# A four-stage decoder trunk on one core: the mixer's work written out as one fixed order on all engines, a narrower overlap, and six more weights split ahead of time

## The chip, the cores and the metric

The kernel runs on one core of a Trainium2 chip. The metric is the device time of one execution in microseconds, the median of several runs; lower is better. The engines are PE (matrix products; PEld is its weight load, which overlaps), DVE (vector), ACT (scalar, with activation functions and running sums), POOL (a second vector engine) and SP, which here only issues DMAs. Each engine runs its own instructions in order, and a DMA that waits on SP holds up those behind it.

## The reference

512 tokens of 1024 channels go through two layers. Every sublayer has a norm in front and behind: x += norm(f(norm(x))), with norm the root-mean-square norm with a gain.

```python
for layer in range(2):
    h = rms_norm(x, mix_pre_g[layer])
    if layer == 0:
        m = pool_mixer(h, pool_w[0], pool_scale[0])      # causal averages over 2, 4, 8, 16 tokens, minus h;
    else:                                                 # then a 256x256 map for each of 4 channel groups
        q = h @ w_q[0]
        o = stick_breaking_attention(q, k, v)             # 16 heads of 64, cumulative products over keys
        m = o @ w_o[0]
    x = x + rms_norm(m, mix_post_g[layer])
    h = rms_norm(x, mlp_pre_g[layer])
    x = x + rms_norm(square(relu(h @ w_up[layer])) @ w_down[layer], mlp_post_g[layer])   # 4096 wide
    if layer == 0:
        k, v = split(rms_norm(x, kv_norm_g) @ w_kv)
```

All is float32, within a tolerance.

## The kernel before, in words

The tokens are four tiles of 128 (t = 0 to 3), the channels eight blocks of 128 (KC), a bank of PSUM holds 128 x 512 numbers and there are eight.

**Products of split operands.** To reach float32 accuracy, a large product takes three passes: each operand is a high part (`hi`, a copy rounded to the fast format, on ACT) and a low part (`lo`, the rest, a subtraction on DVE), and high·high, high·low and low·high are added (`mm3`, lines 255 to 257, and `up_block`, lines 609 to 611). A weight of 128 x 1024 is loaded by `weight` (line 114), copied on ACT (124) and subtracted on DVE (126). An activation tile is transposed on PE (326) and split into `xnh` and `xnl` (`split`, lines 234 and 235).

**Weights ahead of need.** `queue` holds the weights in the order of use; `fill` makes the next one when fewer than `ahead` = 4 wait. In the first MLP, `split_apart` (lines 163 to 186) does the split of 24 weights of the attention stage early: a raw load (176), a gain (135), a cast and a subtraction (184, 185), and one step later two stores into a DRAM tile `kept` (168). Each step advances every weight under way. `steps` (line 518) says after which of the 35 products of the first MLP a step runs. When such a weight is needed, `make` loads its two parts (195) and no split is needed. The raw copies take turns in a tile of three (`apart`), `spare` and `grow`.

**The mixer (lines 614 to 718).** Per tile t: `scaled` squares x on ACT with a running sum (238), takes the reciprocal root with DVE and POOL (`rstd`, lines 244 and 251), and scales x into `xs` (670). `pooled` multiplies by band matrices: eight blocks of 128 x 128 on the tile itself (679) and, for t > 0, eight on the tile before it (684), which bring in the up to 15 tokens that reach over the border; then `y` is copied out (687). `mixed` does the group maps (699), squares the result on ACT (238), multiplies it by the gain on DVE (280), and `add` takes the root and adds to x (286), squaring the new x on ACT. `normed` takes that root and makes `xn` (317). `need` transposes `xn`.

`MIX_ORDER` is the order in which the program text emits these steps; the scheduler then places the instructions of each engine by its own estimate of times, so that only dependencies, and the `issue_after` marks around the steps s, r and w, are given. PE starts with eleven products on zeros (620).

**The first MLP.** `mlp` takes the up products of the first four weights in halves: tokens 0 to 255 as soon as tiles 0 and 1 are transposed, tokens 256 to 511 behind tiles 2 and 3 (lines 551 to 559). The down product of 28 of the 32 blocks goes in five groups (2, 3, 3, 3, 3 pairs), each as seven products of combined operands (`Seven`, line 499): `left` combines activations on POOL (454), `right` combines weights on DVE (473), both are split, and `make(i + 2)` makes the operands two products ahead. The down weights of a group come in two loads, `load(0)` to `w1` and `load(1)` to `xn3` (438). The last four blocks go through `contract`.

**Attention, then the second MLP.** An order written out by hand (`ATT_ORDER`) interleaves projections, heads and the output product; the weights of the output, `o0` to `o7`, are split when they come. The second MLP is built as the first, without `split_apart`.

## Time and profile before

| | us |
|---|---|
| median of three runs | 977.46 (975.99 to 978.87) |
| the profiled execution | 977.16 |
| its span | 975.0 |
| PE busy | 950.8 |
| DVE busy | 709.3 |
| ACT busy | 567.8 |
| POOL busy | 142.3 |

The span runs from the first instruction to the last; 2.2 us lie around it. In rows of the timeline the columns are the start, the time of the row, engine, line, operation, output and inputs, and the number of instructions; in brackets stands the idle time just before and what ended it. Matrix products are pipelined, so the pitch of two rows, not the length of one, is what a product costs. In lists of waits the numbers are the sum, the count and the longest. The granted clock is 1 where PE runs at full speed.

Stages by their marks: the mixer and the first up products from 0 to 77 us, the first MLP to 380, attention to about 604, the output product's end and the second MLP behind it.

### The profile page before, as it was taken

What the parts mean: (1) busy time and instruction counts of PE and PEld (TensorE: products, weight loads), DVE (VectorE), ACT (ScalarE), POOL (GpSimd) and SP (SyncE); (2) the same over time, 40 slices, a digit from 0 to 9 for tenths busy, and PEclk for the clock granted to TensorE, in tenths of its full rate; (3) what the DMA queues carried; (4) which work ended last, traced back from release to release, by engine and by line L of the source; (5) the groups of instructions that cost most, each with busy time, mean ns of one, the idle gap of its engine ahead of it and who ended that gap; (6) DMA issues with size and microseconds to landing.
All of it is one profiled execution on the core that took longest, in us unless ns stands there. A gap on an engine that the chain in (4) does not pass through costs nothing.

```text
span 975.0 us, 12433 instructions
## 1 busy us (share of the span) xinstructions
PE 950.8 (98%) x4795; PEld 807.9 (83%) x4795; DVE 709.3 (73%) x769; ACT 567.8 (58%) x985; POOL 142.3 (15%) x107
## 2 busy tenths in 40 slices
PE   9899999999999999999999998999999999999997
PEld 7798878878888888989799987798888888888886
DVE  3764689796978967376567789875497785957856
ACT  4656788777777546555556574555455454444532
POOL 1102030320403105000000000312040310303003
PEclk8999999999999999999999999999999999999999
DMA  6262767968676540332353312143423324133012
GB/s 251 70 255 72 256 232 275 356 229 303 217 280 227 198 161 1 129 131 87 135 210 118 141 45 87 42 154 109 145 93 128 110 76 163 37 128 115 22 44 87
DMA packets 40092, 144.28 MB, mean 148 GB/s; under 512 B 4065, under 2 KB 4449, under 8 KB 40034
## 3 DMA queue, kind: packets, MB, share of 16 engines
q1 hardware_dynamic: 40034, 143.49, 41.6%
q8 instruction: 38, 0.62, 0.3%
q14 instruction: 20, 0.16, 0.0%
HBM read 116.21 MB, written 27.26 MB: 147 GB/s over the span
## 4 chain that ended last, share of the span: by engine, by line
PE 80%; DVE 8%; ACT 5%; DMA 3%; issue 3%; POOL 1%; DVEq 0%; POOLq 0%; SPq 0%; ACTq 0%
PE ps L499 23%; PE ps L610 12%; PE ps L611 12%; PE ps L609 12%; PE ps L255 4%; PE ps L256 4%; PE ps L257 4%; PE ps L869 2%; PE ps L859 1%; PE ps L699 1%; DMA xn<-in_wdn 1%; DVE w L126 1%; DMA kept<-apart 1%; ACT w L234 1%; PE ps L827 1%
## 5 line engine op out<-in xcount | busy, mean ns | idle before, releaser
L499 PE MATMUL ps<-w,a 128*128 128x512 f32 x1176 | 278.3, 389 | 2.8 <-DVE w L235 1.6
L610 PE MATMUL ps<-xnl,w 128*128 128x512 f32 (+1 forms) x712 | 261.5, 368 | 3.1 <-DVE xnl L235 3.1
L499 PEld LDWEIGHTS ps<-w,a 128*128 128x128 f32 x1176 | 220.5, 188 | 49.8 <-DVE w L235 2.5
L609 PE MATMUL ps<-xnh,w 128*128 128x512 f32 (+1 forms) x712 | 261.1, 368 | 0.4 <-ACT xnh L234 0.3
L611 PE MATMUL ps<-xnh,w 128*128 128x512 f32 (+1 forms) x712 | 261.3, 368 | 0.0
L610 PEld LDWEIGHTS ps<-xnl,w 128*128 128x128 f32 x712 | 134.1, 189 | 25.4 <-DVE xnl L235 3.7
L611 PEld LDWEIGHTS ps<-xnh,w 128*128 128x128 f32 x712 | 134.1, 188 | 22.3
L609 PEld LDWEIGHTS ps<-xnh,w 128*128 128x128 f32 x712 | 133.7, 188 | 22.7 <-ACT xnh L234 0.8
L126 DVE TENSOR_TENSOR w<-raw,w 128x1024 fp32r<-128x1024 f32 x71 | 91.8, 1293 | 66.7 <-ACT w L124 66.6
L124 ACT CAST w<-raw 128x1024 fp32r<-128x1024 f32 x71 | 74.5, 1050 | 107.1 <-PE ps L611 97.4
L508 DVE TENSOR_TENSOR y<-ps,y 128x512 f32<-128x512 f32 x124 | 83.4, 684 | 41.0 <-PE ps L499 41.0
L234 ACT CAST a<-r 128x768 fp32r<-128x768 f32 (+1 forms) x60 | 47.5, 793 | 63.2 <-PE ps L499 46.7
L454 POOL TENSOR_TENSOR s<-r 128x768 f32<-128x768 f32 (+1 forms) x10 | 20.6, 2057 | 371.2 <-ACT r L532 371.2
L234 ACT CAST w<-e 128x1536 fp32r<-128x1536 f32 (+1 forms) x30 | 42.0, 1398 | 46.9 <-DVE e L473 37.5
L235 DVE TENSOR_TENSOR a<-r,a 128x768 fp32r<-128x768 f32 (+1 forms) x60 | 59.9, 1003 | 12.3 <-ACT a L234 12.2
L280 POOL TENSOR_TENSOR y<-y,grow 128x512 f32<-128x512 f32 x12 | 18.8, 1563 | 317.4 <-ACT xn L238 317.4
L454 POOL TENSOR_TENSOR r<-r 128x768 f32<-128x768 f32 (+1 forms) x20 | 52.7, 2635 | 67.2 <-DVE a L235 66.4
L235 DVE TENSOR_TENSOR w<-e,w 128x1536 fp32r<-128x1536 f32 (+1 forms) x30 | 57.5, 1917 | 4.4 <-ACT w L234 4.2
L841 DVE TENSOR_TENSOR_SCAN e<-u,begin 128x1280 f32<-128x1280 f32 x16 | 45.1, 2822 | 12.6 <-ACT u L835 12.3
L135 ACT ACTIVATE apart<-apart,gc 128x128 f32<-128x128 f32 (+1 forms) x132 | 42.8, 405 | 0.0
L238 ACT ACTIVATE xn<-y 128x512 f32<-128x512 f32 (+1 forms) x25 | 15.4, 615 | 39.3 <-DVE y L361 39.2
L235 DVE TENSOR_TENSOR w<-xn,w 128x1536 fp32r<-128x1536 f32 (+1 forms) x20 | 33.0, 1650 | 6.1 <-ACT w L234 6.0
(128 smaller groups left out, 1490.7 us busy)
## 6 DMA issues: line engine op xcount, KB each, us to landing
raw<-in_wup SPq DMA_DIRECT2D x64, 512.0 KB, 3.8
w<-kept SPq DMA_DIRECT2D x48, 512.0 KB, 4.2
w<-in_wdn SPq DMA_DIRECT2D x8, 1536.0 KB, 6.7
kept<-wx SPq DMA_DIRECT2D x24, 512.0 KB, 5.2
xn<-in_wdn SPq DMA_DIRECT2D x8, 1536.0 KB, 7.3
kept<-apart SPq DMA_DIRECT2D x19, 512.0 KB, 3.2
raw<-in_wdn SPq DMA_DIRECT2D x8, 512.0 KB, 4.6
raw<-in_wo SPq DMA_DIRECT2D x8, 512.0 KB, 3.5
```

Of the source, the lines that this page charges most:

```text
L124: nc.scalar.copy(hi, raw)
L126: nc.vector.tensor_tensor(out=lo, in0=raw, in1=hi.bitcast(F32), op=ALU.subtract)
L135: nc.scalar.mul(c, c, gc[:, lo + k : lo + k + 1])
L234: latest["act"] = nc.scalar.copy(hi, src)
L235: latest["dve"] = nc.vector.tensor_tensor(out=lo, in0=src, in1=hi.bitcast(F32), op=ALU.subtract)
L454: sub = lambda out, x, y, op=ALU.subtract: nc.gpsimd.tensor_tensor(out=out, in0=x, in1=y, op=op)
L499: nc.tensor.matmul(bank, a[:, x, q, TS[t]], w[:, z, q], start=start and q == 0 and k == 0, stop=q == self.n - 1 and k == 2, skip_group_che ...
L508: nc.vector.tensor_tensor(out=part, in0=bank, in1=part, op=ALU.add)
L609: nc.tensor.matmul(pu[:, cols], wh[:, k, :], xnh[:, k, cols], start=k == 0, stop=False)
L610: nc.tensor.matmul(pu[:, cols], wh[:, k, :], xnl[:, k, cols], start=False, stop=False)
L611: nc.tensor.matmul(pu[:, cols], wl[:, k, :], xnh[:, k, cols], start=False, stop=k == KC - 1)
L841: nc.vector.tensor_tensor_scan(out=e[:, ::-1], data0=u[:, 1:][:, ::-1], data1=begin[:, ::-1], initial=0.0, op0=ALU.mult, op1=ALU.max,)
```

## The change

- `MIX_ORDER` is a new order, in halves of tiles, and it binds PE, ACT, DVE and POOL (`manual_schedule`). Its letters: q squares, x root and scaling, p pooling (tile, half), m maps, a sum, n norm, t transposes, r and w the gains on the maps, z products on zeros, F the next weight, u the first half of an up product. The first halves of the first four up products move into it (`early`), and `mlp` only does the rest of them. The products on zeros are 8, 6 and 6 instead of 11.
- The squares of x for tiles 1 to 3 are one instruction of 1024 instead of two of 512, with a memset of the second sum.
- The overlap with the tile before takes 16 columns instead of 128.
- `steps` is 1 to 33 without gaps instead of 2 to 30 without 17 and 24; o4 to o7 and the first two up weights of the second MLP are split apart too, without a gain, so 30 instead of 24.
- The raw load of a step is issued behind the latest of `latest["sp"]`, which is now also the store.
- The operands of the first group's first two products are issued behind the latest ACT and DVE work.
- A split up weight may use the fourth slot (`place`).

```diff
 MIX_ORDER = [
-    (w[0], int(w[1])) for w in "s0 r0 s1 w0 p0 p1 w1 s2 m0 s3 m1 p2 F3 n0 p3 t0 n1 t1 m2 F1 m3 n2 n3".split()
+    (w[0], [int(c) for c in w[1:]])
+    for w in """q0 z8 r z6 q1 x0 p00 p01 z6 x1 w0 p10 p11 w1 q2 m00 x2 q3 m01 a0 m10 m11 x3 p20 p21 n0
+    p30 a1 t00 t01 p31 F n1 m20 m21 F t10 t11 u0 a2 m30 F m31 u1 n2 a3 F t20 t21 u2 n3 F u3""".split()
 ]
...
-            fourth = count[0] % 4 == 0 and k[0] in "vkqo"
+            fourth = k[0] in "vkqo" and count[0] % 4 == 0 or k[0] == "up" and k[2] == GRP - 1
...
             for n, t in enumerate((hi.bitcast(F32), raw)):
-                nc.sync.dma_start(kept[k][n], t)
+                latest["sp"] = nc.sync.dma_start(kept[k][n], t)
...
-            nc.sync.dma_start(raw, src)
+
+            with tc.issue_after(latest["sp"].ins) if "sp" in latest else nullcontext():
+                nc.sync.dma_start(raw, src)
             going.append([k, 0, raw, None, scaled])
...
             if n == 1:
-                scaled(raw)
+                if scaled is not None:
+                    scaled(raw)
...
-            apart.extend(x for x in queue[n:] if x[0][0] != "o")
+            apart.extend(x for x in queue[n:] if x[0] not in [("o", c) for c in range(4)])
+            apart.extend((("up", 1, j), wup[1, j], None) for j in range(2))
...
-        def transpose(self):
-            for h in range(2):
+        def transpose(self, halves=range(2)):
+            for h in halves:
...
-        steps = [n for n in range(2, 31) if n not in (17, 24)] if l == 0 else []
+        steps = [n for n in range(1, 34)] if l == 0 else []
...
-        first = [(ps(), get(("up", l, j))) for j in range(n0)]
+        first = early[:]
+        while len(first) < n0:
+            first.append((ps(), get(("up", l, len(first)))))
         for j, (pu, w) in enumerate(first):
             if j == n0 - 1:
                 need(2, 3)
                 groups[0].load(1)
-            up_block(pu, w, slice(0, S // 2))
+            if j >= len(early):
+                up_block(pu, w, slice(0, S // 2))
+        early.clear()
...
-        for i in range(2):
-            groups[0].make(i)
+        with tc.issue_after(latest["act"].ins), tc.issue_after(latest["dve"].ins):
+            for i in range(2):
+                groups[0].make(i)
...
+        def busy(n):
+            for _ in range(n):
+                nc.tensor.matmul(pwarm, warm[:, :P], warm, start=True, stop=True)
...
+        def squares(t):
+            xs[t] = mp.tile([P, D], F32, tag=f"xs{t}", name=f"xs{t}")
+            sts[t] = keep.tile([P, 8], F32, tag=f"stat{t}", bufs=4, name=name("stat"))
+            if t == 0:
+                for n in range(2):
+                    square_sum(xt[t][:, NS[n]], xs[t][:, NS[n]], sts[t], n)
+            else:
+                nc.vector.memset(sts[t][:, 1:2], 0.0)
+                square_sum(xt[t], xs[t], sts[t], 0)
...
+        def pooled(t, h):
...
+                if t:
+
+                    n = max(WINDOWS)
                     nc.tensor.matmul(
-                            py[:, TS[c]], xs[t - 1][:, cs], band(2, cb // 2), start=False, stop=True
+                        py[:, c * P : c * P + n], xs[t - 1][:, cs], band(2, cb // 2)[:, :n], start=False,
+                        stop=True, skip_group_check=True,
                     )
...
+        def half_up(j):
+            early.append((ps(), get(("up", 0, j))))
+            up_block(*early[j], slice(0, S // 2))
+
+        steps = {
+            "q": squares, "x": scaled, "p": pooled, "m": mixed, "a": lambda t: ups[t].add(), "n": normed,
+            "t": transposed, "r": spread, "w": linear, "F": fill, "z": busy, "u": half_up,
+        }
+        on = mybir.EngineType
+        with tc.manual_schedule(engines={on.PE, on.Activation, on.DVE, on.Pool}):
+            for step, which in MIX_ORDER:
+                steps[step](*which)
```

More of the change, by code (lines that the diff above doesn't have):

```diff
@@ L617, in trunk @@
         nc.gpsimd.memset(warm, 0.0)
-        pwarm = ps()
-        for _ in range(11):
-            nc.tensor.matmul(pwarm, warm[:, :P], warm, start=True, stop=True)
         cst = mp.tile([P, 12 * P], F32, tag="cst", name="cst")
@@ new lines, in scaled @@
+        def scaled(t):
+            r = rstd(sts[t], 0)
+            for n in NS:
+                nc.vector.tensor_scalar(out=xs[t][:, n], in0=xt[t][:, n], scalar1=r, scalar2=None, op0=ALU.mult)
+        def pooled(t, h):
+            if not h:
+                ys[t] = mp.tile([P, D], F32, tag="y", bufs=2, name=f"y{t}")
+            py = ps()
+            for c in range(4):
+                cb = 4 * h + c
+                cs = slice(cb * P, (cb + 1) * P)
+                nc.tensor.matmul(
+                    py[:, TS[c]], xs[t][:, cs], band(0 if t == 0 else 1, cb // 2), start=True, stop=True,
+                    skip_group_check=True,
+                )
+                if t:
+                    n = max(WINDOWS)
@@ L706, in normed, with transposed @@
             pending[t] = ups[t]
[L708 to L718 removed]
+        def transposed(t, h):
+            ups[t].transpose((h,))
+            if h:
+                pending.pop(t)
+        def half_up(j):
[9 more added lines that the diff above has]
+                steps[step](*which)
     with tc.tile_pool(name="mlp0", bufs=1, reuse_waits="tile") as mp:
```

67 lines of the change are left out of this document (19 added, 48 removed).

## The prediction

> **What bounds the kernel now.** I read the page's busy shares first, then the waits of PE, then the timeline around each wait.
>
> ```profile
> PE 950.8 (98%) x4795; PEld 807.9 (83%) x4795; DVE 709.3 (73%) x769; ACT 567.8 (58%) x985; POOL 142.3 (15%) x107
> ```
>
> PE is idle for 975.0 − 950.8 = 24.2 us in all, so whatever removes no PE work can save at most this. The waits of PE, longest first, say who ends that idle time:
>
> ```profile
> PE ps L679 <- DVE xs L670: 4.5, 2, 3.9
> PE ps L610 <- DVE xnl L235: 3.1, 3, 2.1
> PE ps L256 <- DVE w L126: 2.1, 2, 1.9
> PE ps L499 <- DVE w L235: 1.6, 2, 1.0
> ```
>
> All four name DVE. Their places are the mixer (L679), the borders into the second MLP and of the last heads (L610, L256), and the first MLP (L499). The second thing that costs is the clock. In the windows the columns are length, busy time of PE, PEld, DVE, ACT and POOL, granted clock, DMA share and GB/s:
>
> ```profile
> 0.00:75.00 75.00, 68.36 (x431) 60.91 (x432) 44.63 (x74) 40.04 (x85) 7.92 (x19) 0.93 0.52 187
> 10.00:15.00 5.00, 4.41 (x21) 4.12 (x20) 4.05 (x10) 0.79 (x3) 0.51 (x1) 0.50 0.99 388
> 30.00:35.00 5.00, 3.52 (x22) 3.56 (x23) 4.34 (x7) 1.72 (x4) 0.55 (x1) 0.77 0.48 145
> 250.00:275.00 25.00, 25.00 (x112) 20.68 (x112) 25.00 (x21) 20.62 (x40) 9.77 (x4) 1.00 0.63 214
> ```
>
> So the mixer has 75 − 68.36 = 6.6 us of idle PE and two stretches at half clock, and in 250 to 275 us DVE is busy all the time.
>
> **Part 1: the mixer in a fixed order.** These PE rows give its pitches:
>
> ```profile
> 1.31 4.56 PE L620 MATMUL ps<-warm 128*128 128x512 bf16 x11 [1.31 <-POOL warm L617]
> 16.92 7.07 PE L699 MATMUL ps<-pw,y 128*128 128x256 f32 x32
> 23.83 0.39 PE L679 MATMUL ps<-cst,xs 128*128 128x128 f32 x2
> 24.05 0.39 PE L684 MATMUL ps<-cst,xs 128*128 128x128 f32 x2
> 31.48 0.46 PE L679 MATMUL ps<-cst,xs 128*128 128x128 f32 x2 [3.91 <-DVE xs L670]
> 36.75 1.91 PE L326 MATMUL ps<-ident,xn 128*128 128x128 f32 x16
> 57.62 0.28 PE L611 MATMUL ps<-xnh,w 128*128 128x256 f32 x1
> 57.74 0.28 PE L609 MATMUL ps<-xnh,w 128*128 128x256 f32 x1
> ```
>
> A 128-column pooling product takes 24.05 − 23.83 = 0.22 us, half a tile of the group maps 7.07/4 = 1.77, half a tile of transposes 4 × 0.11 = 0.44 (sixteen in 1.91, the last with its tail), a warm-up product 4.56/11 = 0.41. Half an up product is 24 × (57.74 − 57.62) = 2.88, and five of them from 57.40 on end the mixer's share at about 72. The other engines, in the same stage:
>
> ```profile
> 18.85 0.60 ACT L238 ACTIVATE xn<-ps 128x512 f32<-128x512 f32 x1
> 37.43 2.06 ACT L234 CAST xnh<-ps 128x512 fp32r<-128x512 f32 x4
> ```
>
> ```profile
> 19.57 0.69 DVE L280 TENSOR_TENSOR m<-ps,grow 128x512 f32<-128x512 f32 x1 [0.39 <-ACT xn L238]
> 35.60 1.23 DVE L126 TENSOR_TENSOR w<-raw,w 128x1024 fp32r<-128x1024 f32 x1 [0.55 <-ACT w L124]
> 38.06 2.48 DVE L235 TENSOR_TENSOR xnl<-ps,xnh 128x512 fp32r<-128x512 f32 x4 [1.23 <-ACT xnh L234]
> 44.35 1.41 DVE L286 SCALAR_TENSOR_TENSOR x<-m,stat,x 128x512 f32<-128x512 f32 x2 [0.66 <-POOL stat L251]
> ```
>
> A tile's norm has the form of its sum (two of 128x512, 1.41). Each reciprocal root goes from DVE to POOL and back, and DVE stands 0.66 us for it. I laid the new order end to end with these durations, each step beginning when its engine and its operands are ready.
> - Tiles 0 and 1 come 3.2 us earlier (second maps end at 20.6 against 23.8), if the 20 warm-ups in place of 11 (9 × 0.41 at half clock, in time in which PE waits for x and its root anyway) spare the half clock of 10 to 15 us.
> - Tile 3's pooling then waits for xs3: DVE does both of tile 1's gain products first, and reaches it at 25.1. PE is idle from 23.3 to 25.7 (2.4), where before it was idle 3.9 until 31.5.
> - Tile 1's transposes wait for its norm: x at 29.1, squares to 31.2, root and norm to 36.6. PE has tile 2's maps until 33.7, then idles 3.0.
> - u0 needs the low halves of tile 1, behind tile 2's gains and a weight split on DVE: first product at 38.0, the rest at 40.3 (2.0 idle).
> - Tile 2's norm, tile 3's sum, a weight split, the two low halves of tile 2 and tile 3's norm follow on DVE without a break, so t3 begins at 58.7 and the four second halves (4 × 2.88) end at 72.0.
>
> Before, that last product ends at about 72 too. The order changes what PE does while DVE works, and DVE's chain sets the end in both; it reaches tile 3's norm at 58 instead of 53, and what covers this is that all four first halves are done.
>
> The 16-column overlap removes 112 of 128 columns in 24 products of two instructions each. A 16-column price is not in the trace. Nearest are two bounds in the last heads' products:
>
> ```profile
> 594.64 0.22 PE L869 MATMUL ps<-ah,v 128*128 128x128 f32 x1
> 594.70 0.28 PE L869 MATMUL ps<-al,v 128*128 128x128 f32 x1
> ```
>
> The pitch there is 0.06 per instruction, against 0.11 in the mixer: 24 × 2 × 0.05 = 2.4 us at best and 0 at worst. I take 0.06, in the 72.0 above; at 0.11 the end is 72.8. [...]
>
> The clock is what the laid rows leave out. Before, the 3.91 us idle before 31.48 was followed by half clock in 30 to 35. The new gaps from 33.7 to 40.3 hold 6.6 us with only 1.2 us of PE work, so I expect 3.4 us of half clock on u0 and tile 3's maps: these are on the path, and the end moves to 73.7. Of 3.4 us at half clock 1.7 is lost. The same behind the gap at 23.3 costs nothing, since tile 1's norm covers it. If the half clock of 10 to 15 us stays as well, the end is 75.4. [...]
>
> Mixer: **+1.7 us** (0 with full clock, +4.2 with the early half clock and 0.11 a product).
>
> **Part 2: six more splits in the first MLP.** Each is 1.13 of DVE and 0.95 of ACT, a load, two stores of 512 KB. 6 × 1.13 = 6.8 us of DVE and 12 × 0.5 MB of stores and reads lie beside PE, except where DVE is full. The two steps that were left empty fall in the window 250 to 275, where DVE shows 25.00 of 25. A split there delays the next operand by up to 1.13; part of it is caught up, since operands are made two products ahead: I take +0.7 for both.
> The loads behind stores matter here:
>
> ```profile
> 175.42 0.33 SPq L176 DMA_DIRECT2D apart<-in_wk  x1
> 176.28 0.42 SPq L438 DMA_DIRECT2D xn<-in_wdn  x1
> ```
>
> ```profile
> 185.14 2.12 DVE L473 TENSOR_TENSOR e<-xn,w 128x1536 f32<-128x1536 f32 x1 [3.88 <-DMA xn<-in_wdn]
> ```
>
> ```profile
> 129.92 1.45 PE L499 MATMUL ps<-w,a 128*128 128x512 f32 x5 [0.64 <-DVE w L235]
> 196.31 0.96 PE L499 MATMUL ps<-w,a 128*128 128x512 f32 x3 [1.00 <-DVE w L235]
> 201.18 1.20 PE L499 MATMUL ps<-w,a 128*128 128x512 f32 x4 [1.17 <-DVE a L235]
> ```
>
> ```profile
> SPq L176 <- DMA kept<-apart: 43.6, 14, 6.4
> ```
>
> SP stands 43.6 us at raw loads that wait for an earlier store. One of them, at 175.42, holds the down-weights' load (176.28); DVE then waits 3.88 for it, and PE loses 1.00 and 1.17 behind that. In the new order the raw load stands behind the stores, and the down-weights' load comes ahead of it: −2.2. What SP queues behind a waiting raw load is now the next up weight's load, with up to four weights made ahead of it (ahead, line 139). MLP 0: **−1.5 us** (−2.8 with the 0.64 at 129.9 too; +4.4 if each filled step gives a pair of stalls like the one above).
>
> **Part 3: what the later stages lose.** o4 to o7 and two up weights arrive split, so their casts and splits go, and each load becomes two of 512 KB.
>
> ```profile
> 592.67 0.50 PE L256 MATMUL ps<-w,ohl 128*128 128x512 f32 x1 [1.93 <-DVE w L126]
> 597.85 0.49 PE L869 MATMUL ps<-ah,v 128*128 128x512 f32 x1 [0.35 <-ACT ah L234]
> 599.18 0.50 PE L869 MATMUL ps<-al,v 128*128 128x512 f32 x1 [0.84 <-DVE al L235]
> 633.96 0.39 PE L610 MATMUL ps<-xnl,w 128*128 128x256 f32 x1 [2.15 <-DVE xnl L235]
> 646.39 0.38 PE L610 MATMUL ps<-xnl,w 128*128 128x256 f32 x1 [0.45 <-DVE xnl L235]
> ```
>
> ```profile
> 597.31 1.21 DVE L126 TENSOR_TENSOR w<-raw,w 128x1024 fp32r<-128x1024 f32 x1
> 629.74 1.23 DVE L126 TENSOR_TENSOR w<-raw,w 128x1024 fp32r<-128x1024 f32 x1
> 630.88 2.42 DVE L286 SCALAR_TENSOR_TENSOR x<-y,stat,x 128x512 f32<-128x512 f32 x2
> ```
>
> The 1.93 is o3's split, and o3 is not among the six: it stays. The split at 597.31 is o6's or so and goes: −0.35 − 0.84 = −1.2. At 633.96 the split of 629.74 goes from the chain (−1.13), and tile 1's low half comes ahead of tile 2's sum; but what is late next is tile 3's norm, which then stands behind tile 2's low halves, and its products begin within 0.2 us of where they did (646.4): no more than +0.2. **−1.0 us** (−4.3 if all stalls quoted here but 1.93 go; +1 if the split loads come late, each waiting for one of four slots).
>
> **Sum.** +1.7 − 1.5 − 1.0 = −0.8 on the profiled execution's 977.16 us, which stands 0.3 below the median: 976.7 us.
>
> **Rivals.**
> - Faster: the clock holds in the mixer (it is granted again sooner when the warm-ups end later; against it, 5.5 idle us between 33.7 and 40.3), and the stalls of part 2 and most of part 3 go: 0 − 2.2 − 3 = −5.2, 972.3 us.
> - Slower, at the filled steps: DVE, 25.00 of 25 busy, makes two groups' operands late as at 196 and 201, 2 × 2.2 = +4.4 in place of −1.5: 982.6 us. It decides once a split delays an operand by more than the two products (2 × 2.2 us) it is made ahead; against it, over the whole span DVE is 27% free.
> - Slower, in the mixer: with PE only 16.8 of 26 us busy between 34 and 60 (4 × 2.88 of first halves, 3.5 of maps, 4 × 0.44 of transposes), the clock stays at half until t3 instead of for 3.4 us. The laid rows then end at 81.2, 7.5 later: 984.2 us. It decides if the clock isn't back by u1. Against it: the mean of 0.77 in 30 to 35 says that the half clock there took half of five us, not all.
> - The change does not do what it says: the later stalls are latency between engines (0.66 per root) and not split work, so they stay, and the mixer's 1.7 is left with nothing but the −0.8 of part 2: 978.5 us.
>
> **How the numbers follow.** A measurement of this kernel tells about 0.3% (2.9 us) from nothing. Forecast and the last rival, both within 2.9 of 977.46: 0.27 and 0.12. Faster rival: 0.33. Slower rivals: 0.16 and 0.12. Faster than 974.6: 0.33; within: 0.39; slower than 980.4: 0.28. The likeliest by sign is not the likeliest case: 976.7 is given, its own range (bounds of part 1 with 2 and 3) 974 to 980. The range reaches to 971.5 (the faster rival and 0.8 more for 0.64 at 129.9) and to 982.8, which leaves out the rest of the slow mixer (0.12) and a corner at the low end.
>
> **What would show it.** Right: the page still has PE at 97 to 98%; no half clock in 10 to 15, but 0.5 to 0.8 somewhere in 38 to 46; the first L499 product near 78.7 against 77.0; the L176 wait on kept<-apart gone from SP; no L499 stall near 196 to 201; an L256 stall near 2 us still before the last heads. Wrong: a clock of 1.00 throughout 30 to 60 (faster); L499 stalls near 250 to 275 (slower); the L610 stall before tile 2 of the second MLP unchanged (part 3 fails).

## The result, and the profile after

The changed kernel takes 983.74 us (median of 20 executions, 977.39 to 986.52) against 976.96 for the kernel before (20 executions on the same chip): 1.0057 times as long, 95% interval 1.0041 to 1.0074. It is slower, where 976.7 was forecast with 982.8 as the upper end of the range. Its times fall into two groups, nine from 977.4 to 980.3 and eleven from 983.0 to 986.5; those of the kernel before spread evenly over 975.5 to 978.9. The profiled execution took 986.38, so it is one of the upper group.

The changed kernel's page and its list of PE's waits (sum, count, longest):

```profile
PE 959.1 (97%) x4804; PEld 812.2 (82%) x4804; DVE 715.6 (73%) x772; ACT 566.9 (58%) x979; POOL 138.5 (14%) x107
```

```profile
PE ps L334 <- DVE xn L325: 6.1, 3, 3.3
PE ps L507 <- DVE a L243: 2.4, 3, 0.9
PE ps L264 <- DVE w L130: 2.1, 2, 1.9
PE ps L623 <- DVE xnl L243: 1.9, 1, 1.9
```

PE's idle time is 984.6 − 959.1 = 25.5 us, 1.3 more than before; but PE is busy 8.3 us longer with nearly the same products. Nine more on zeros are 2.9 us of this; the other 5.4, over half of the loss, is time in which PE is busy and slow. Windows of the changed kernel (the granted clock is the number ahead of the DMA share):

```profile
44.00:50.00 6.00, 5.28 (x24) 5.28 (x25) 2.80 (x6) 1.39 (x4) 0.55 (x1) 0.50 0.29 91
600.00:603.00 3.00, 3.00 (x8) 2.35 (x8) 2.04 (x4) 0.00 (x0) 0.00 (x0) 0.50 0.57 175
652.00:655.00 3.00, 3.00 (x16) 3.00 (x15) 1.59 (x3) 1.91 (x3) 0.00 (x0) 0.50 0.14 23
```

Three stretches at half clock: at u0 and tile 3's maps (6.8 us long), at the last heads (3.4) and in front of the second MLP (6.8). The kernel before has none of the last two. In the profiles of both kernels the changes of the granted clock lie whole multiples of 3.413 us apart: half clock from 43.34 to 50.17, 599.72 to 603.13 and 650.92 to 657.74 here, from 8.83 to 15.66 and 32.72 to 36.14 before. The stretches of half clock read in the experiments fit this (3.4, 6.8, 10.2 and 13.7 us). A span of 3.413 us that begins and ends whole multiples of it from such a change is called a window below. The clock's record begins with the first change, so the half clock at the start must be read from the pitch of rows. Rows of the changed kernel on PE:

```profile
4.84 3.78 PE L662 MATMUL ps<-row,ones 1*128 1x512 f32 x4
8.55 2.74 PE L656 MATMUL ps<-warm 128*128 128x512 bf16 x6
14.90 0.39 PE L698 MATMUL ps<-cst,xs 128*128 128x128 f32 x2
15.12 0.29 PE L705 MATMUL ps<-cst,xs 128*128 128x16 f32 x2
15.27 0.47 PE L698 MATMUL ps<-cst,xs 128*128 128x128 f32 x2
15.57 0.29 PE L705 MATMUL ps<-cst,xs 128*128 128x16 f32 x2
18.39 7.15 PE L720 MATMUL ps<-pw,y 128*128 128x256 f32 x32
41.13 1.38 PE L334 MATMUL ps<-ident,xn 128*128 128x128 f32 x8 [2.24 <-DVE xn L325]
44.72 0.58 PE L623 MATMUL ps<-xnl,w 128*128 128x256 f32 x1 [1.88 <-DVE xnl L243]
84.31 1.07 PE L507 MATMUL ps<-w,a 128*128 128x512 f32 x4
599.67 0.78 PE L264 MATMUL ps<-w,ohl 128*128 128x512 f32 x1 [1.93 <-DVE w L130]
651.69 1.94 PE L334 MATMUL ps<-ident,xn 128*128 128x128 f32 x8 [3.28 <-DVE xn L325]
```

The same places of the kernel before, as far as they were not shown:

```profile
5.80 1.98 PE L647 MATMUL ps<-row,ones 1*128 1x512 f32 x4
76.99 2.88 PE L499 MATMUL ps<-w,a 128*128 128x512 f32 x12
```

The spread of the scale (the products of one row, with input `row`, that copy it to all partitions) takes 3.78 us instead of 1.98, and the six products on zeros behind it 2.74 where the six at 13.61 take 1.46: half clock until about 12.6. The first down product (the mark used below for the mixer's end) comes 84.31 − 76.99 = 7.3 us later. From there to the attention's first product with `ohl` (a tile of the heads' split outputs) the changed kernel is 0.3 faster, from that to the last one it takes as long as before (156.8), and behind it it loses 2.6 more: 7.3 − 0.3 + 2.6 = 9.6, the difference of the spans.

### The profile page after: what moved, and what is told of

It is laid out like the page before. It is cut to its first block, busy times and chain, and to the rows that moved or that the text cites. A ratio compares the mean times of both kernels' runs of the same rounds, so it can differ in the third digit from the quotient of the medians.

```text
span 984.6 us, 12507 instructions
## 1 busy us (share of the span) xinstructions
PE 959.1 (97%) x4804; PEld 812.2 (82%) x4804; DVE 715.6 (73%) x772; ACT 566.9 (58%) x979; POOL 138.5 (14%) x107
## 4 chain that ended last, share of the span: by engine, by line
PE 82%; DVE 8%; ACT 4%; issue 2%; DMA 2%; POOL 1%; POOLq 0%; DVEq 0%; ACTq 0%
PE ps L507 24%; PE ps L623 13%; PE ps L624 13%; PE ps L622 13%; PE ps L264 4%; PE ps L265 4%; PE ps L263 4%; DMA xn<-in_wdn 2%; PE ps L895 2%; DVE w L130 2%; PE ps L885 1%; DVE w L243 1%; PE ps L853 1%; PE ps L854 1%; ACT xn L246 1%
## 5 line engine op out<-in xcount | busy, mean ns | idle before, releaser
L507 PE MATMUL ps<-w,a 128*128 128x512 f32 x1176 | 278.4, 389 | 2.4 <-DVE a L243 2.4
L507 PEld LDWEIGHTS ps<-w,a 128*128 128x128 f32 x1176 | 220.5, 188 | 49.4 <-DVE a L243 3.7
L623 PEld LDWEIGHTS ps<-xnl,w 128*128 128x128 f32 x712 | 136.3, 191 | 24.3 <-DVE xnl L243 2.5
L624 PEld LDWEIGHTS ps<-xnh,w 128*128 128x128 f32 x712 | 136.2, 191 | 23.2 <-DVE w L130 1.0
L622 PEld LDWEIGHTS ps<-xnh,w 128*128 128x128 f32 x712 | 135.8, 191 | 22.8 <-ACT w L128 0.6
L130 DVE TENSOR_TENSOR w<-raw,w 128x1024 fp32r<-128x1024 f32 x66 | 83.9, 1271 | 60.2 <-ACT w L128 60.2
L128 ACT CAST w<-raw 128x1024 fp32r<-128x1024 f32 x66 | 69.0, 1047 | 84.7 <-PE ps L624 79.0
L243 DVE TENSOR_TENSOR a<-r,a 128x768 fp32r<-128x768 f32 (+1 forms) x60 | 60.0, 1003 | 14.6 <-ACT a L242 14.5
L462 POOL TENSOR_TENSOR r<-r 128x768 f32<-128x768 f32 (+1 forms) x20 | 48.7, 2437 | 64.5 <-DVE a L243 49.7
L867 DVE TENSOR_TENSOR_SCAN e<-u,begin 128x1280 f32<-128x1280 f32 x16 | 45.2, 2822 | 13.3 <-ACT u L861 13.0
```

The lines of the kernel that those rows point to most:

```text
L128: nc.scalar.copy(hi, raw)
L130: nc.vector.tensor_tensor(out=lo, in0=raw, in1=hi.bitcast(F32), op=ALU.subtract)
L243: latest["dve"] = nc.vector.tensor_tensor(out=lo, in0=src, in1=hi.bitcast(F32), op=ALU.subtract)
L462: sub = lambda out, x, y, op=ALU.subtract: nc.gpsimd.tensor_tensor(out=out, in0=x, in1=y, op=op)
L507: nc.tensor.matmul(bank, a[:, x, q, TS[t]], w[:, z, q], start=start and q == 0 and k == 0, stop=q == self.n - 1 and k == 2, skip_group_che ...
L622: nc.tensor.matmul(pu[:, cols], wh[:, k, :], xnh[:, k, cols], start=k == 0, stop=False)
```

## The experiments

Fourteen kernels were run. The mark "first product" is the first row of L499 (L502, L507, L509) in the first MLP; it follows the mixer by the same work in all of them, so its differences are the mixer's. Each ratio is to the kernel before on the same chip; each profile is one execution.

### The two halves of the change, each alone

`mix_only` is the changed kernel with the splits of before:

```diff
-            apart.extend(x for x in queue[n:] if x[0] not in [("o", c) for c in range(4)])
-            apart.extend((("up", 1, j), wup[1, j], None) for j in range(2))
+            apart.extend(x for x in queue[n:] if x[0][0] != "o")
...
-        steps = [n for n in range(1, 34)] if l == 0 else []
+        steps = [n for n in range(2, 31) if n not in (17, 24)] if l == 0 else []
...
-                latest["sp"] = nc.sync.dma_start(kept[k][n], t)
+                nc.sync.dma_start(kept[k][n], t)
...
-            with tc.issue_after(latest["sp"].ins) if "sp" in latest else nullcontext():
-                nc.sync.dma_start(raw, src)
+            nc.sync.dma_start(raw, src)
```

> The new mixer with the old 24 splits, the old steps and the raw loads issued as before. Theory M (the loss is made in the mixer, at the clock): nearly all of the difference of the changed kernel's profile up to 380 us, +7.0, is here: about +7 against before, first L499 product near 84.3, and the later stages as in the kernel before, so 983 to 985. Rival S (the new splits cost it): the mixer by itself even with before, within 2 us.

`split_only` is the kernel before with these lines (and the slot of `place`) as in the changed one.

> The old mixer with the 30 splits, all 33 steps and the raw loads behind stores. Theory M: the first MLP is even to 0.4 us better than before, and behind the heads the idle time of PE goes from 4.3 to about 3.3, so -1 to 0 against before when the clock holds there; +3 to +5 when PE is throttled behind the two idle stretches (near 592 and 644), so two groups of times. Rival S: +4 to +7 in all executions.

Measured: mix_only 986.55, ratio to before 1.0103 (1.0090 to 1.0116); split_only 976.23, ratio 0.9993 (0.9982 to 1.0004). The loss is made in the mixer, as theory M has it, though mix_only came out above its 983 to 985; the splits are worth nothing measurable in the median. In mix_only the start is as slow as in the changed kernel, and the clock comes 1.2 us later still, at 13.8:

```profile
4.95 3.75 PE L660 MATMUL ps<-row,ones 1*128 1x512 f32 x4
19.01 7.15 PE L718 MATMUL ps<-pw,y 128*128 128x256 f32 x32
```

In split_only the first MLP is 1.1 us shorter than before, and behind the heads this stands (a row of PE and a window):

```profile
640.23 1.94 PE L329 MATMUL ps<-ident,xn 128*128 128x128 f32 x8 [3.71 <-DVE xn L320]
```

```profile
640.00:643.00 3.00, 2.77 (x13) 2.80 (x14) 1.61 (x4) 1.17 (x2) 0.00 (x0) 0.50 0.00 0
```

The idle times of 0.35, 0.84, 2.15, 0.53 and 0.45 of the kernel before are one of 3.71 in front of tile 3's transposes, and half clock follows it.

What the splits are worth in the later stages can be read over all the profiles. From the attention's first product with `ohl` to the last one, nine profiles with the new splits take 155.3 us; the four that have a window of half clock at the last heads take 156.6 to 156.8, and the kernel before takes 156.8. From there to the second MLP's first down product it is 35.5 to 35.7 in the four profiles without half clock there (three with the old splits, and split_fill_late), 36.3 to 36.7 with one window of it (nine profiles), and 37.7 to 38.0 with two (three). So the new splits save 1.6 us in the attention stage as long as the clock holds, and half clock takes this back: as much at the last heads, and about 1.1 for each window in front of the second MLP.

### The clock at the start and at u0

`full_row` makes the spread a product of 128 rows, 127 of them zero:

```diff
-        one_row = mp.tile([1, D], F32, tag="row", name="row")
-        ones = mp.tile([1, P], F32, tag="ones", name="ones")
+        one_row = mp.tile([P, D], F32, tag="row", name="row")
+        ones = mp.tile([P, P], F32, tag="ones", name="ones")
+        nc.vector.memset(one_row, 0.0)
...
-        nc.sync.dma_start(one_row, grow[R_SCALE : R_SCALE + 1, :])
+        nc.sync.dma_start(one_row[0:1, :], grow[R_SCALE : R_SCALE + 1, :])
```

> The changed kernel, with the product that spreads the scale over the partitions done with 128 rows (127 of them zero) instead of one; the DVE fills the zeros at the start. Theory R (a product of one row counts as idle for the clock gate, so the spread of 3.78 us keeps PE at half clock until 12.1): full clock from 5.4 on, the spread in about 2 us, first map near 14 to 15 instead of 18.4, the first L507 product 3 to 4 us sooner. Rival W (the eight products ahead of it, ending at 4.9, are too few to open the gate, whatever follows): half clock until 8.8 or later, gain under 2 us.

`fill_gap` puts products on zeros into PE's idle time around tile 1's transposes:

```diff
-    ... m20 m21 F t10 t11 u0 ...
+    ... m20 m21 z8 F t10 t11 z6 u0 ...
```

> The changed kernel, with 8 products on zeros ahead of tile 1's transposes and 6 behind them, where PE is idle for 2.2 and 1.9 us. Theory G (the idle time there takes the clock for 6.8 us from 42.8, on the path): clock 1.00 from 12.1 to 75, the first L507 product about 3 us sooner than 84.3. Rival (DVE's chain ends the mixer, and the clock of PE there is hidden): under 1 us.

Measured: full_row 980.91, ratio 1.0052 (1.0033 to 1.0070); fill_gap 980.43, ratio 1.0041 (1.0023 to 1.0060). In full_row's profile (978.82) the clock came at 4.0, while the eight products on zeros still ran: here they were not too few (rival W), and since the spread came behind, the profile says nothing for or against theory R. Its first map stands at 14.62 and its first product at 79.61. One of its six executions is still at 986.2. The profile of fill_gap is one of its faster executions (977.02), and it shows more than it was made for. Its start is the changed kernel's, instruction for instruction:

```profile
4.88 2.15 PE L662 MATMUL ps<-row,ones 1*128 1x512 f32 x4
14.84 7.15 PE L720 MATMUL ps<-pw,y 128*128 128x256 f32 x32
78.33 1.07 PE L507 MATMUL ps<-w,a 128*128 128x512 f32 x4
```

Here the clock came at about 5.3, the spread took 2.15, and the maps began at 14.84 instead of 18.39. So the same code starts in two ways, 3.6 us apart, and what differs is when the clock comes, at 5.3 or at 12.6. That this is one source of the two groups fits the ten profiles with the fixed order: the three with the first map at 18.4 or later are of executions of 985.6 to 986.4, the seven with it at 14.6 to 15.8 of 976.2 to 982.2. The changed kernel itself has no profile in the lower group. In the profiles of kernels with this start the clock comes at 5.3 (fill_gap), or 7 to 9 us later, at 12.6 to 14.0 (the changed kernel, mix_only, and after_128 below). With the fillers no half clock is left between 5.3 and 643, and the first product stands at 78.33: still 1.3 later than before, whose own half clock stands in that number. fill_gap's expectation on the first product (3 us) is met together with the start's share; the two are told apart by the map's row, 3.55 of the 5.98 us, so that 2.4 is left for the gap.

`full_fill` is both edits together.

> The changed kernel with the spread on 128 rows and the fillers ahead of and behind tile 1's transposes. If the two stretches at half clock make all of the mixer's loss: the first L507 product near 78 in nearly all executions (the laid schedule at full clock ends 1.3 later than before), so 976 to 979 with what the last stages lose to the clock, and no group above 983. Rival (the fixed order itself costs more): 980 or more also where no half clock shows up to 75 us.

Measured: 979.35, ratio 1.0025 (1.0012 to 1.0039), twelve executions from 976.1 to 982.2 and none in the upper group; the median is 0.35 above the 976 to 979 that were expected. Its profile, of the slowest execution, has a window that ends in the middle of the spread:

```profile
5.05 3.06 PE L663 MATMUL ps<-row,ones 128*128 128x512 f32 x4
```

The clock came at about 7.3, behind a window filled by products on zeros until 4.9 and by the spread for the rest. In mix_only a window that ended at nearly the same time, 7.0, with the one-row spread in its second part, was followed by half clock until 13.8. A second pair bears on the same: the kernel before and split_fill (below, with the spread on 128 rows) both get the clock at 5.4, behind the same eleven products, and both go on with the spread and tile 0's pooling. The kernel before loses the clock again at 8.8; split_fill keeps it, though PE is idle for 1.71 us in the next window:

```profile
5.69 1.88 PE L655 MATMUL ps<-row,ones 128*128 128x512 f32 x4
```

```profile
8.50:11.50 3.00, 1.29 (x11) 1.10 (x10) 1.19 (x4) 2.07 (x6) 0.55 (x1) 1.00 0.98 365
```

So theory R holds as far as two pairs of profiles show: with the spread of one row PE is as busy in the record, but the clock came later (13.8 against 7.3) or was lost again (at 8.8, where split_fill kept it). It is not always lost: in fill_gap the clock stayed full from 5.3 on, behind a window that was half filled by the one-row spread (to 7.03), with products on zeros behind it. full_fill's profile has half clock from 27.8 to 34.6 all the same, behind the wait for tile 3's xs (1.39), which neither edit fills, and its first product stands at 80.81, not near 78:

```profile
27.80:34.50 6.70, 6.66 (x32) 6.69 (x33) 4.06 (x9) 2.82 (x7) 1.09 (x2) 0.50 0.00 0
```

`lean` has the products on zeros as before (eleven ahead of the spread, none behind):

```diff
-    ... q0 z8 r z6 q1 x0 p00 p01 z6 x1 ...
+    ... q0 z9 z2 r q1 x0 p00 p01 x1 ...
```

> The changed kernel with its products on zeros as in the kernel before: eleven at the start, none behind the spread. Theory P (PE's start at half clock depends on where the gate's windows of 3.4 us fall; eleven products fill a window more often, and no products on zeros stand ahead of tile 0's pooling when the clock is half): the first map starts between 14.5 and 17 in place of 14.8 or 18.4, and most executions fall in the lower group, 977 to 981. Rival (the products on zeros behind the spread are what holds the clock): the first map at 17 or later, 981 to 985.

Measured: 982.53, ratio 1.0053 (1.0036 to 1.0070), executions from 978.8 to 987.4. The profile (979.90) has its first map at 14.57, in the range that theory P gave, but the executions do not gather in the lower group, as theory P had it: four of twelve are below 981. The number of products on zeros alone does not hold the start together; no profile shows one of the slower executions.

### The 16 columns

`before_16` is the kernel before with the narrow overlap alone:

```diff
-                        start=True, stop=t == 0,
+                        start=True, stop=True, skip_group_check=True,
...
-                            py[:, TS[c]], xs[t - 1][:, cs], band(2, cb // 2), start=False, stop=True
+                            py[:, c * P : c * P + 16], xs[t - 1][:, cs], band(2, cb // 2)[:, :16], start=False,
+                            stop=True, skip_group_check=True,
```

> The kernel before with nothing but the overlap narrowed to 16 columns. Theory of the prediction (0.06 per instruction): the pooling of tile 2 takes 2.8 us instead of 3.6, up to 2.4 us less PE work. Theory L (the load of 128 weight columns sets the pace; in the changed kernel a pair of 128 and 16 columns still takes 0.445): 3.56 us for tile 2's pooling as before, and no change in the time beyond 0.1%.

Measured: 984.53, ratio 1.0077 (1.0060 to 1.0095). Neither theory had this: the edit that saves work costs 7 us by itself. Rows and a window of before_16:

```profile
25.47 0.38 PE L679 MATMUL ps<-cst,xs 128*128 128x128 f32 x2
25.69 0.29 PE L684 MATMUL ps<-cst,xs 128*128 128x16 f32 x2
25.83 0.47 PE L679 MATMUL ps<-cst,xs 128*128 128x128 f32 x2
39.93 3.65 PE L326 MATMUL ps<-ident,xn 128*128 128x128 f32 x16
82.38 2.88 PE L499 MATMUL ps<-w,a 128*128 128x512 f32 x12
```

```profile
31.00:44.00 13.00, 10.89 (x50) 10.83 (x51) 7.92 (x11) 6.13 (x11) 1.10 (x2) 0.50 0.37 122
```

A narrow product takes 0.14, but the wide one behind it 0.30, so a pair takes 0.44 to 0.45, exactly as with 128 columns: nothing is saved. The rows of the weight loads on PEld fit theory L: each product's two loads are of 128 columns in the changed kernel too, and they begin 0.22 us behind the last product's, at 15.02, 15.24 and 15.46 there and at 23.95, 24.17 and 24.39 in the kernel before. That the loads set the pace is not shown beyond this. What the narrow products do change is the clock. In the kernel before the half clock behind the 4 us wait for xs3 lasts one window, 3.4 us (32.72 to 36.14), and is over before the end of tile 3's pooling (36.75). In before_16 that pooling runs from 33.1 to 39.9 at half clock and the clock stays at half from 30.4 to 44.0, four windows, over the transposes (3.65 instead of 1.91) into the maps. The first product comes at 82.38 instead of 76.99. Of these 5.4 us, 1.6 stand before tile 2's pooling (25.47 against 23.83): here the early half clock, two windows in both, fell from 13.3 to 20.2, over the first maps, instead of 8.8 to 15.7. The first MLP takes 1.7 longer in this profile; how far that is the edit's is open.

A pair whose half clock starts at the same time is split_only and split_16_o3 (below), with 128 and with 16 columns. Both lose the clock at 28.6; with 128 columns it is back at 35.5, with 16 at 38.9, one window later, and the first product stands at 76.38 instead of 74.82. Windows of split_only, then of split_16_o3:

```profile
28.70:35.40 6.70, 6.01 (x28) 6.04 (x29) 4.83 (x8) 1.99 (x4) 0.55 (x1) 0.50 0.53 158
28.70:38.80 10.10, 9.46 (x45) 9.49 (x46) 5.51 (x10) 3.69 (x7) 0.55 (x1) 0.50 0.51 157
```

So the narrow products lengthen the half clock in both pairs. That the whole 7 us of the median comes by this path is not shown: each kernel has one profile.

`after_128` undoes the same in the changed kernel (`n = P` for `n = max(WINDOWS)`).

> The changed kernel with nothing but the overlap at 128 columns again. In the kernel before, 16 columns alone cost 7 us, through half clock in the pooling and behind it. Theory U (in the fixed order the loss is made before the pooling, at the start, and at tile 1's transposes, so the 16 columns matter little there): 0 to 3 us faster than the changed kernel, 980 to 984, with two groups of times again. Rival N (the narrow products are what loses the clock in the fixed order too): back within 2 us of the kernel before, 976 to 979.

Measured: 983.06, ratio 1.0066 (1.0052 to 1.0081), as the changed kernel itself (1.0057), so theory U holds against rival N: undoing the 16 columns gains nothing here. In the changed kernel's profile the clock is full from 12.6 to 43.3, over all of the pooling. That is not a rule of the fixed order, though: of the other five profiles of it with 16 columns, four (mix_only, full_row, full_fill and lean) have one or two windows of half clock from 28 or 31 on, over tile 3's pooling, and of the four with 128 columns none has.

`split_16_o3` is split_only with the 16 columns and o3 split apart too (31 weights, `range(1, 35)`).

> The mixer's order of before, with the 16 columns, the new splits and o3 split apart as well (31 weights, 34 steps). Theory: the idle 1.93 us ahead of o3's first products goes, since it was o3's split behind the scans, and PE idles less than 0.5 there: 1.9 us below the kernel with the splits alone (976.2), so 974 to 975. Rival: the next wait there (the heads' transposed weights on DVE) takes its place, no gain.

Measured: 981.68, ratio 1.0043 (1.0021 to 1.0064), 974.9 to 986.7, where 974 to 975 was expected: the narrow products again, in the pair of windows above. On o3 the rival is right, for the wait has only another name now, v's split behind the same scan on DVE:

```profile
591.04 0.33 PE L873 MATMUL ps<-ah,v 128*128 128x128 f32 x1 [2.06 <-DVE v L748]
```

### The order at equal clock

`after_128_fill` is the changed kernel with 128 columns, the full-row spread and the fillers.

> The changed kernel with 128 columns, the spread on 128 rows and the fillers at tile 1's transposes: full clock from 8.2 at the latest to 75. Expected from the laid schedule at full clock: first L507 product near 78, 976 to 979 in all executions, so 2 us below the one with the same fillers and 16 columns (979.35) in its middle. Rival: 979 again, since what is left is the half clock behind the idle times near 592 and 645.

`split_fill` is split_only with the full-row spread, PE's order of the mixer written out as it was, and 16 products on zeros while PE waits for tile 3's xs:

```diff
-    (w[0], int(w[1])) for w in "s0 r0 s1 w0 p0 p1 w1 s2 m0 s3 m1 p2 F3 n0 p3 t0 n1 t1 m2 F1 m3 n2 n3".split()
+    (w[0], int(w[1])) for w in "s0 r0 s1 w0 p0 p1 w1 s2 m0 s3 m1 p2 F3 n0 z8 z8 p3 t0 n1 t1 m2 F1 m3 n2 n3".split()
...
+        fixed = ctx.enter_context(ExitStack())
+        fixed.enter_context(tc.manual_schedule(engines={mybir.EngineType.PE}))
         for step, t in MIX_ORDER:
...
+        fixed.close()
```

> The kernel before with the new splits, the spread on 128 rows, PE's order in the mixer as it was, and 16 products on zeros in the 3.9 us in which PE waits for tile 3's xs. If the clock is what the old mixer loses: no half clock between 9 and 37, the first L502 product at 72 to 74 in place of 76.99, and 972 to 975, faster than both kernels. Rival (DVE's chain hides it): 975 to 977.

Measured: after_128_fill 978.44, ratio 1.0016 (1.0007 to 1.0025), all eleven executions from 977.0 to 979.7; split_fill **971.70**, ratio 0.9949 (0.9933 to 0.9965). Neither profile has half clock between 6 and 630. Against full_fill, after_128_fill differs by the 128 columns alone: 1.0016 against 1.0025 with overlapping intervals, so the 2 us expected of them were not seen in the median. First products, after_128_fill and then split_fill:

```profile
78.55 1.07 PE L507 MATMUL ps<-w,a 128*128 128x512 f32 x4
```

```profile
25.22 3.62 PE L625 MATMUL ps<-warm 128*128 128x512 bf16 x16
71.12 2.88 PE L502 MATMUL ps<-w,a 128*128 128x512 f32 x12
```

At equal, full clock the fixed order ends 78.55 − 71.12 = 7.4 us later than the old one; the medians differ by 6.7. The two seemed even in the prediction because the old one was read with its half clock in it (76.99), and the new one laid without. split_fill differs from split_only by three things (the full-row spread, the filler, PE's bound order), which were not run one by one. Two reasons for the 7.4 were tried.

`roots` issues each reciprocal root one or two DVE steps ahead of its use (letters d, b, c for the roots of x, sum and norm; 128 columns, full-row spread, filler behind t11 only). Beside the roots it moves x3 ahead of tile 1's maps and tile 0's sum, that sum between the two maps, and a2 ahead of u0:

```diff
-    ... w1 q2 m00 x2 q3 m01 a0 m10 m11 x3 p20 p21 n0 p30 a1 t00 t01
-    p31 F n1 m20 m21 F t10 t11 u0 a2 m30 F m31 u1 n2 a3 F t20 t21 u2 n3 F u3
+    ... w1 q2 d2 m00 x2 q3 d3 m01 x3 b0 m10 a0 m11 p20 p21 b1 c0 n0 p30 a1 t00 t01
+    p31 c1 F n1 m20 m21 b2 F t10 t11 z8 a2 u0 m30 c2 m31 b3 F u1 n2 a3 c3 F t20 t21 u2 n3 F u3
...
```

> The changed kernel with 128 columns and the spread on 128 rows, and the same steps, but each reciprocal root is issued one or two DVE steps ahead of its use (fillers only behind tile 1's transposes). Theory D (DVE stands 0.66 for POOL at each of twelve roots, 8 us in the changed mixer against 4 before, and this chain ends the mixer): laid with the same durations, the end comes 4.3 sooner; first L507-type product near 74 in place of 78.5, 973 to 975. Rival (these waits lie beside others): first product at 77 or later, 977 to 979.

`m3_first` moves tile 3's maps ahead of tile 1's transposes and u0 (`m20 m21 m30 m31 F t10 t11 z6 u0 a2 F u1 a3 n2 ...`; 128 columns, full-row spread).

> The changed kernel with 128 columns and the spread on 128 rows, with tile 3's maps ahead of tile 1's transposes and of u0 instead of behind u0. Theory Q (PE's order holds tile 3 back): tile 3's maps at about 35 instead of 44, first L507-type product 4 us or more sooner than 78.5. Theory D (DVE's chain): no more than 1.1 us sooner, since DVE reaches tile 3's sum no earlier; 977 to 979.

Measured: roots 976.60, ratio 0.9993 (0.9980 to 1.0006), even with before and between the two expectations; m3_first 980.09, ratio 1.0032 (1.0019 to 1.0046). DVE's waits for POOL up to 75 us, in the changed kernel, in roots, and in the kernel before:

```profile
DVE xs L689 <- POOL stat L259: 2.7, 4, 0.7
DVE xn L325 <- POOL stat L259: 2.7, 4, 0.7
DVE x L294 <- POOL stat L259: 2.7, 4, 0.7
```

```profile
DVE xs L692 <- POOL stat L259: 1.3, 2, 0.7
DVE xn L327 <- POOL stat L259: 1.1, 1, 1.1
```

```profile
DVE x L286 <- POOL stat L251: 1.4, 3, 0.7
DVE xs L670 <- POOL stat L251: 1.3, 2, 0.7
DVE xn L317 <- POOL stat L251: 1.3, 2, 0.7
```

Twelve waits of 0.67, 8.1 us, in the fixed order; 4.0 before, where the scheduler put other work between a root and its use; 2.4 in roots, whose first product is 3.2 us sooner. First products of roots and of m3_first, and what took the place of the maps' delay in the latter:

```profile
75.39 1.07 PE L509 MATMUL ps<-w,a 128*128 128x512 f32 x4
```

```profile
52.06 1.75 PE L334 MATMUL ps<-ident,xn 128*128 128x128 f32 x8 [3.74 <-DVE xn L325]
78.93 1.07 PE L507 MATMUL ps<-w,a 128*128 128x512 f32 x4
```

The place of tile 3's maps in PE's order is not it: with them out of the way PE waits 3.74 for tile 2's norm on DVE. A window of half clock follows that wait (52.4 to 55.8) and can cost up to 1.7, half its length, so at full clock m3_first gains at most some 1.3 us against 78.55, and not the 4 of theory Q. roots regains 3.2 of the 7.4 us, mostly by the roots as far as the waits tell, but its moved steps were not run alone; the other 4.2 were not taken apart further and stay open.

### The clock in front of the second MLP

`split_fill_late` adds to split_fill fourteen products of the identity between the transposes of tiles 2 and 3:

```diff
+                if l == 1:
+                    need(2)
+                    with tc.manual_schedule(engines={mybir.EngineType.PE}):
+                        pz = ps()
+                        for _ in range(14):
+                            nc.tensor.matmul(pz[:, :P], ident, ident, start=True, stop=True)
                 need(2, 3)
```

> The kernel split_fill with 14 products of the identity between the transposes of tiles 2 and 3 in front of the second MLP, where PE is idle for 3.71 us. Theory H (that idle time takes the clock for 3.4 or 6.8 us): no half clock between 630 and 660, 1.7 to 3.4 us faster, 968 to 970. Rival (the clock there is taken by idle time elsewhere, or is not on the path): 971 to 972.

Measured: **969.41**, ratio 0.9927 (0.9912 to 0.9941), the fastest of all. The window behind that place, in split_fill and in split_fill_late:

```profile
634.00:640.00 6.00, 5.39 (x26) 5.42 (x27) 2.51 (x4) 1.17 (x2) 0.00 (x0) 0.50 0.38 106
```

```profile
634.00:640.00 6.00, 5.41 (x47) 5.07 (x46) 4.15 (x8) 2.52 (x7) 0.55 (x1) 1.00 0.14 40
```

Half clock there is gone, and that stage is shorter: from the last product with `ohl` to the second MLP's first down product it takes 35.56 us (622.53 to 658.09) instead of 37.93 (619.99 to 657.92), 2.4 less, as theory H had it. The ratio is 0.2% lower, 2 us, but the two intervals overlap between 0.9933 and 0.9941, and the two profiled executions have equal spans (967.3 and 967.5), since the first MLP took 2.5 longer in the latter. So the gain of the stage is shown, and that of the whole kernel is not settled.

## Why the prediction was wrong

The term that failed most is the mixer's: +7.3 in the profiled execution in place of +1.7. Of this, 3.55 is the half clock at the start, 2.4 that at u0, and 1.3 is what the fixed order at full clock (fill_gap) is later than the old one with its half clock. The later stages lost 2.6 in place of gaining 1.0.

- **"The 20 warm-ups spare the half clock of 10 to 15" failed**, and it is the largest miss. Eight products end at 4.9, the one-row spread behind them runs at half clock (3.78 us), and in the profile the clock comes at 12.6 (again at 15.66 before, where the products on zeros end at 5.87). The prediction put this case at 1.7 us; by the first map it is 3.55, since the six products on zeros behind the spread then stand on PE's path too (tile 0's pooling follows them at 11.09, though its xs was ready by 7). In fill_gap the same code escaped it (the clock came at 5.3).
- **The half clock at u0 was foreseen, its length was not**: 6.8 us (43.34 to 50.17) in place of 3.4, and 2.4 on the path in place of 1.7. The 3.4 was the author's estimate: the kernel before has it behind its wait of 3.91 (32.72 to 36.14), but no run shows it as a fixed length, and behind such waits the changed kernel has 3.4 once and 6.8 twice.
- **The 16 columns save nothing**: the value taken, 0.06 per instruction from the row at 594.64, failed, and the other end of the bound, 0 us and an end at 72.8, held. The pooling pair keeps its 0.111 an instruction (0.445 for four); the row is one of another kind of product (the rounded format, not plain float32), and why that one is faster was not tested. What the bound did not reach is a cost: alone, in the old order, the narrow products cost 7 us, at least in part through the clock. In the changed kernel undoing them gains nothing (after_128).
- **"Before, that last product ends at about 72 too" hid the order's own price.** At full clock the old order's first product comes at 71.1 and the new one's at 78.4. The loss at half clock in the old mixer, about 5.9 us, was not counted as something that both orders could lose or be rid of.
- **First MLP, −1.5**: −0.3 in the changed kernel and −1.1 in split_only, and both are within what executions differ by: from the first product to the first with `ohl` it is 396.7 before, and 393.6 to 398.3 in the profiles with the new splits. So a gain of 1.5 is neither shown nor ruled out. The down-weights' load did move ahead of the raw load, and DVE's wait of 3.88 for it fell to 0.89 (row below); but DVE's splits now delay an operand three times, 2.4 us together (L507 in the list of waits) for the 2.8 before. The rival of 2 × 2.2 at the filled steps did not come in the changed kernel's profile, but a pair of such waits stands in two profiles with the new splits: 1.15 and 1.41 at 265 and 270 in after_128, inside the stretch that the prediction named, and 1.21 and 1.40 at 322 and 325 in full_fill.

```profile
190.27 1.76 DVE L481 TENSOR_TENSOR e<-xn,w 128x1536 f32<-128x1536 f32 x1 [0.89 <-DMA xn<-in_wdn]
```

- **Later stages, −1.0**: the 1.93 stayed and the 0.35 and 0.84 went, as said. Tile 3's norm is late next, as said, and the sum of idle times, 3.28 for 3.13, is as predicted. That one long idle time does to the clock what three short ones did not was missed: two windows of half clock follow it (650.92 to 657.74), 2.2 us by the stage. The window near 600 follows the 1.93 that stands in both kernels, and takes back the 1.6 that the splits save there. The sum has no term for the clock in these stages, and gives no reason for that.
- **The rival "slower, in the mixer"** named the right mechanism at 984.2 with a chance of 0.12: the measured median is 983.74. That the number is so near is luck: it expected the half clock from u0 to t3 in one piece, 7.5 us more; it came at the start, for 6.8 us at u0 and in the late stages, and the fixed order's own price is in the sum too.
- **Small slips of the sums**, without effect here: the last rival is 977.46 + 1.7 − 0.8 = 978.4, not 978.5; the idle time between 33.7 and 40.3 is given as 6.6 − 1.2 = 5.4 and as 5.5, and is 5.0 by its two gaps; and the −4.3 of part 3 is 3.8 by the rows that stand there, the rest being the wait of 0.53 before 644.

## What to carry to other kernels

Where PE waits in pieces of one and a half to four us (half clock followed waits of 1.39 in full_fill, 1.93 in the changed kernel and 3.91 in the kernel before), price a change by the clock it leaves behind, not by the idle time: compare the laid schedules of both kernels at the same clock, and then add the half clock to both. Cheap products in a wait that nothing else fills, with the spread on 128 rows, went with the fastest kernels here (972 and 969 us against 977), where the reordering gained nothing; products that are narrow, or one row deep, did that duty less well (half clock for 10.2 us in split_16_o3 against 6.8 in split_only, and until 13.8 in mix_only against 7.3 in full_fill). An order written out by hand for DVE must also say what stands between a root on POOL and its use, which the scheduler had found by itself.

## What the runs showed of the hardware

- A pooling product of 16 columns behind one of 128 takes 0.14, and the pair 0.445, as two of 128. In the old order the half clock lasted one window longer with it (28.6 to 38.9 in split_16_o3, 28.6 to 35.5 in split_only).
- The stretches of half clock were multiples of 3.413 us long (3.4, 6.8, 10.2, 13.7), and where they fall against the kernel's start differs from profile to profile: the first full clock of the same start came at 5.3 (fill_gap) or at 12.6 (the changed kernel). The changed kernel's two groups of times lie about 5 us apart; the start accounts for 3.6 of it.
- A wait of 1.93 us at the last heads stands in both kernels; half clock followed it in the changed kernel's profile and not in that of before, and in some of the experiments' profiles and not in others. Where its border lies was not measured.
